# The decode attention's 16 products go from GpSimd to VectorE and start one weight tile later

## The chip, the cores and the metric

The kernel runs on one core of one Trainium2 chip. A core has TensorE (PE, with its weight loads shown as PEld), VectorE (DVE), ScalarE (ACT), GpSimd (POOL) and SyncE (SP). Each engine works through its own instruction stream in order and waits on semaphores for the others. Here SP only issues DMAs. The metric is the device time of one execution in microseconds (us), smaller being better; the median of several runs is compared. The trace of one execution shows instructions, what each waited for, the clock granted to TensorE, and DMA traffic.

## What is computed

One step of a two-layer decoder, for a prompt group (1024 tokens) and a sample group (8 sequences with one new token each) that share the weights. Layer 0 puts dilated window attention and a state space scan side by side; layer 1 is a matrix memory mixer. The change touches one piece of layer 0: the attention of the 8 new tokens over their cached keys and values.

```python
def dilated_attention_sample(q, k, v, k_buf, v_buf):
    kk = jnp.concatenate([k_buf.astype(k.dtype), k], axis=1)
    vv = jnp.concatenate([v_buf.astype(v.dtype), v], axis=1)
    ...
    for window, dil in DILATION_PATTERNS:
        ...
        s = jnp.einsum('bthe,btjhe->bthj', q, kg, preferred_element_type=jnp.float32)
        s = jnp.where(valid[None, :, None, :], s, -jnp.inf)
        lse = jax.nn.logsumexp(s, axis=-1)
        p = jnp.exp(s - lse[..., None])
        outs.append(jnp.einsum('bthj,btjhe->bthe', p.astype(v.dtype), vg))
        lses.append(lse)
    return combine_by_denominator(outs, lses)
```

In the kernel a partition holds one of 64 pairs of sequence and head, with one of two halves of the cached rows that any pattern reaches: 128 partitions, 128 rows each, 64 values per row. All is float32.

## The kernel before, in words

Layer 0 runs in this order. First the q, k and v projections (tiles `pq`). Then a loop over 12 weight tiles f of the state space branch (L698 on). For each f it takes a weight tile `w` (loaded by SP to `raw`, L95; rounded by ScalarE to `wh`, L90; the remainder `wl` by VectorE, L91), runs three column blocks c of 24 matmuls each (`pf`, L112), copies them out on ScalarE (`craw`, L242), and then runs a 4-tap convolution: the first tap on ScalarE (L248), three on VectorE (L250), the activation on ScalarE (L254) with its product on VectorE (L255). After it a second loop of 12 tiles (gates), in which the state space scan runs (`sE`, from L730), then the output projection.

Two other streams are handed out between the column blocks of the first loop:

- `att_pump` steps, only in f = 0 to 5, and the rest in one go at f = 5: the prompt attention's remaining blocks. TensorE makes scores `pS` (L428); VectorE adds the mask and finds the extremum (L433, reading PSUM); ScalarE takes the exponential (L434); statistics `ast` go through DRAM and back as `aot` (L441 to L443); VectorE combines them (`aft`, L448 to L456) and scales the probabilities `P` (L468); TensorE transposes them (`pT`, L470); VectorE or ScalarE copies them to `PT` (L475, L473); TensorE multiplies with the values (`pO`, L487).
- `dpump` steps, one per column block: the decode attention, 19 steps in the queue `dq`. `dec_prep` loads the new queries, keys and values (`q_b`, `k_b`, `v_b`, L628). Eight `dec_k` steps each load 128 x 1024 cached keys to `dk` (L632), multiply them in place with the query (L634, GpSimd) and sum over 64 values (L635, VectorE) to 16 scores of `dsc`. `dec_soft` makes the softmax. Eight `dec_v` steps do the like with the cached values, `dv` (L649), the product with the probabilities (L651, GpSimd) and the sum over 128 rows (L652, VectorE). `dec_fin` joins the halves through DRAM.

The tiles `dk`, `dv` and later `sE` share one pool of three buffers (tag "E"), so a fourth load waits until a sum has released a buffer; all these loads go out on SP in SP's order. The result is read by `dec_fin2` (L676, tile `pda`) at f = 1 of the second loop.

The order of a queue is not the order in which the code emits: the framework plans each engine's stream ahead, takes an instruction when its operands are ready in its plan and the engine is free there, and among several ready ones the earliest in the code. So steps that depend on little stand far ahead of their place in the code. The position in the code acts as a rank.

Of the kernel before, what the change touches and what calls it, by code (L numbers as in the profile page):

```python
# [28 lines left out]
def body(ctx, tc, I, O):  # L29
    nc = tc.nc  # L30
    V, A, G, PE = nc.vector, nc.scalar, nc.gpsimd, nc.tensor
    mult, add, sub, mx, mn = ALU.mult, ALU.add, ALU.subtract, ALU.max, ALU.min
# [23 lines left out]
    def S(name, dt=F32):  # L56
        return slab.tile([128, 1040], dt, tag="S", name=name)
# [4 lines left out]
    def EP(name, dt=F32):  # L62
        return cur["ep"].tile([128, 1040], dt, tag="E", name=name)
# [19 lines left out]
    def C(name, shape, src=None, p=None):  # L83
        t = (p or cur["cst"]).tile(shape, F32, name=name)
        if src is not None:
            load(t, src)
        return t
# [27 lines left out]
    class Weights:  # L115
# [8 lines left out]
        def load(self, ahead=1):  # L124
            while len(self.raws) < min(ahead, len(self.srcs)):
                self.raws.append(raw_load(*self.srcs[len(self.raws)]))
# [112 lines left out]
    def conv_c(w, xh, xl, c, raw, samp, side=()):  # L239
        p = proj_c(w, xh, xl, c, side)  # L240
        if c < 2:
            A.copy(raw[:, 3 + c * CH : 3 + (c + 1) * CH], p[:, :CH])  # L242
        else:
            A.copy(raw[:, 3 + 2 * CH : 3 + NP], p[:, : CH - 8])
            A.copy(samp, p[:, CH - 8 : CH])

    def conv_taps(raw, o, w4, b1, tail):
        A.activation(o[:, :NP], raw[:, 0:NP], AF.Identity, bias=b1, scale=w4[:, 0:1])  # L248
        for j in range(1, 4):
            V.scalar_tensor_tensor(o[:, :NP], raw[:, j : j + NP], w4[:, j : j + 1], o[:, :NP], mult, add)  # L250
        G.tensor_scalar(tail, raw[:, NP : NP + 3], 1.0, None, mult)

    def conv_act(raw, o):
        A.activation(raw[:, :NP], o[:, :NP], AF.Tanh)  # L254
        V.scalar_tensor_tensor(o[:, :NP], raw[:, :NP], 1.0, o[:, :NP], add, mult)  # L255

    def conv_raw(raw=None):
        raw = S("craw") if raw is None else raw
        G.memset(raw[:, 0:3], 0.0)
        return raw  # L260
# [250 lines left out]
    def att_pump(n, limit):  # L511
        for _ in range(n):
            if attq and attq[0][0] < limit:
                attq.popleft()[1]()
# [80 lines left out]
    def dt_prep():  # L595
        V.tensor_tensor(dtr, dtr, dtb.unsqueeze(1).broadcast_to([128, 9, 16]), add)
        softplus_neg(dtf, 144, False)
        A.activation(alog, alog, AF.Exp)
        V.tensor_scalar(alog, alog, -1.0, None, mult)
        V.tensor_tensor(dta, dtr, alog.unsqueeze(1).broadcast_to([128, 9, 16]), mult)  # L600
        pac = X("pac")
        PE.matmul(pac[:, 0:128], tri, dtaf[:, 0:128], start=True, stop=True)
        PE.matmul(pac[:, 128:256], ones, dtaf[:, 0:128], start=True, stop=True)
        PE.matmul(pac[:, 256:384], dtaf[:, 0:128], tri, start=True, stop=True)
        V.tensor_copy(acum, pac[:, 0:128])
        V.tensor_scalar(nacum, acum, -1.0, None, mult)
        V.tensor_tensor(wl, pac[:, 128:256], acum, sub)
        A.activation(wl, wl, AF.Exp)
        V.tensor_tensor(wl, wl, dtf[:, 0:128], mult)
        A.activation(dec, pac[:, 128:256], AF.Exp)  # L610
        act_sb = smg.tile([128, 128], F32, tag="dg", name="act_sb")
        V.tensor_copy(act_sb, pac[:, 256:384])
        store(acd, act_sb)
# [3 lines left out]
    q_b = C("q_b", [128, 64])  # L617
    k_b = C("k_b", [128, 64])
    v_b = C("v_b", [128, 64])
    dsc = C("dsc", [128, 129])  # L620
# [9 lines left out]
    def dec_k(j):  # L630
        t = EP("dk")
        load(t[:, :1024], I["ck"][:, j * 1024 : j * 1024 + 1024])  # L632
        tv = t[:, :1024].rearrange("p (a b) -> p a b", b=64)
        G.tensor_tensor(tv, tv, q_b.unsqueeze(1).broadcast_to([128, 16, 64]), mult)  # L634
        V.reduce_sum(dsc[:, j * 16 : j * 16 + 16], tv, AX.X)  # L635

    def dec_soft():
# [9 lines left out]
    def dec_v(j):  # L647
        t = EP("dv")
        load(t[:, :1024], I["cv"][:, j * 1024 : j * 1024 + 1024])  # L649
        tv = t[:, :1024].rearrange("p (a b) -> p a b", b=128)  # L650
        G.tensor_tensor(tv, tv, dsc[:, 0:128].unsqueeze(1).broadcast_to([128, 8, 128]), mult)  # L651
        V.reduce_sum(dao[:, j * 8 : j * 8 + 8], tv, AX.X)  # L652

    def dec_fin():
# [23 lines left out]

    dq = deque([dec_prep])
    dq.extend(lambda j=j: dec_k(j) for j in range(8))  # L680
    dq.append(dec_soft)
    dq.extend(lambda j=j: dec_v(j) for j in range(8))
    dq.append(dec_fin)

# [3 lines left out]
    def dpump(n):  # L688
        for _ in range(n):
            if dq:  # L690
                dq.popleft()()
# [7 lines left out]
    for f in range(12):  # L699
        w = wq0.next()  # L700
        raw = conv_raw()
        o = S("cout")
        for c in range(3):
            conv_c(w, xh, xl, c, raw, xbs[:, f])
            if c == 1 and later:
                later.popleft()()
            if f < 6:
                att_pump(3, 4)
            if f > 3:
                dpump(1)  # L710
        conv_taps(raw, o, scw[:, f], scb[:, f : f + 1], cvo[:, f])
        later.append(lambda raw=raw, o=o: conv_act(raw, o))
        xbc.append(o)
        if f == 5:
            att_pump(80, 4)
        if f == 7:
            dt_prep()
# [1146 lines left out]
```

## Time and profile before

| | |
|---|---|
| median of 3 runs | 2164.42 us (2162.53 to 2165.84) |
| the profiled execution | 2158.71 us, of which the span of the trace is 2156.9 us |
| PE busy | 2097.2 us, 97% of the span |
| DVE busy | 1350.3 us, 63% |
| ACT busy | 849.6 us, 39% |
| POOL busy | 561.9 us, 26% |
| mean granted TensorE clock | 0.994 of full speed |

How to read it: times are from the span's start. Busy is the time in which at least one instruction of the engine ran. A bracket behind an instruction tells how long its engine stood idle just before it and what ended that. A clock of 1.00 is the upper of the two levels, 2.4 GHz, and 0.50 is the lower, 1.2 GHz; a figure between is a mean over a stretch that has both. A wait for several semaphores is put down to the one that came last.

### The profile page before, as it was taken

What the parts mean: (1) busy time and instruction counts of PE and PEld (TensorE: products, weight loads), DVE (VectorE), ACT (ScalarE), POOL (GpSimd) and SP (SyncE); (2) the same over time, 40 slices, a digit from 0 to 9 for tenths busy, and PEclk for the clock granted to TensorE, in tenths of its full rate; (3) what the DMA queues carried; (4) which work ended last, traced back from release to release, by engine and by line L of the source; (5) the groups of instructions that cost most, each with busy time, mean ns of one, the idle gap of its engine ahead of it and who ended that gap; (6) DMA issues with size and microseconds to landing.
All of it is one profiled execution on the core that took longest, in us unless ns stands there. A gap on an engine that the chain in (4) does not pass through costs nothing.

```text
span 2156.9 us, 35181 instructions
## 1 busy us (share of the span) xinstructions
PE 2097.2 (97%) x12926; PEld 1880.9 (87%) x12926; DVE 1350.3 (63%) x3176; ACT 849.6 (39%) x1837; POOL 561.9 (26%) x1052
## 2 busy tenths in 40 slices
PE   7999989999999999999999999999999999999998
PEld 6877777997898899989989899898898998987798
DVE  7444388768778655645548566575565665746844
ACT  5434334454425434433425334253343443524421
POOL 4222144015540002142141321413214223141000
PEclk9999999999999999999999999999999999999999
DMA  4222053125555552411214133132231232416852
GB/s 160 72 73 78 26 156 97 47 94 169 184 169 179 178 178 77 99 40 47 89 34 151 44 97 116 37 115 78 84 131 29 92 106 68 142 30 199 280 169 94
DMA packets 162076, 232.29 MB, mean 108 GB/s; under 512 B 41200, under 2 KB 106976, under 8 KB 161904
## 3 DMA queue, kind: packets, MB, share of 16 engines
q1 hardware_dynamic: 161904, 230.04, 34.0%
q8 instruction: 102, 1.67, 0.3%
q14 instruction: 70, 0.57, 0.1%
HBM read 174.35 MB, written 55.62 MB: 107 GB/s over the span
## 4 chain that ended last, share of the span: by engine, by line
PE 78%; DVE 7%; DMA 3%; POOL 3%; issue 2%; ACT 2%; POOLq 0%; SPq 0%; DVEq 0%; ACTq 0%
PE pf L112 32%; PE pvo L112 16%; PE po L931 14%; PE pq L112 4%; PE mN L112 2%; PE mC L112 2%; PE pS L428 1%; PE pO L487 1%; PE mS L1294 1%; PE pT L470 1%; DMA sE<-acd 1%; POOL mCl L91 1%; DVE P L468 1%; PE mH L1355 1%; PE mS L1296 1%
## 5 line engine op out<-in xcount | busy, mean ns | idle before, releaser
L112 PE MATMUL pf<-yh,wh 128*128 128x344 f32 x1152 | 370.1, 321 | 0.0
L112 PE MATMUL pf<-yl,wh 128*128 128x344 f32 x1152 | 368.9, 320 | 0.0
L112 PE MATMUL pf<-yh,wl 128*128 128x344 f32 x1152 | 368.5, 320 | 0.0
L91 DVE TENSOR_TENSOR wl<-raw,wh 128x1024 fp32r<-128x1024 f32 x128 | 161.7, 1263 | 156.3 <-ACT wh L90 155.7
L90 ACT CAST wh<-raw 128x1024 fp32r<-128x1024 f32 x128 | 133.9, 1047 | 254.8 <-PE pf L112 93.6
L112 PEld LDWEIGHTS pf<-yh,wh 128*128 128x128 f32 x1152 | 216.9, 188 | 1.3 <-ACT craw L242 1.0
L112 PEld LDWEIGHTS pf<-yl,wh 128*128 128x128 f32 x1152 | 216.5, 188 | 0.0
L112 PEld LDWEIGHTS pf<-yh,wl 128*128 128x128 f32 x1152 | 216.4, 188 | 0.0
L112 PE MATMUL pvo<-wvh,yh 128*128 128x512 f32 x512 | 206.0, 402 | 0.0
L112 PE MATMUL pvo<-wvh,yl 128*128 128x512 f32 x512 | 201.9, 394 | 0.0
L112 PE MATMUL pvo<-wvl,yh 128*128 128x512 f32 x512 | 201.7, 394 | 0.0
L112 PE MATMUL pf<-xh,wh 128*128 128x344 f32 x576 | 195.4, 339 | 0.8 <-ACT gth L236 0.8
L112 PE MATMUL pf<-xh,wl 128*128 128x344 f32 x576 | 188.0, 326 | 0.0
L112 PE MATMUL pf<-xl,wh 128*128 128x344 f32 x576 | 187.9, 326 | 0.0
L1282 DVE TENSOR_SCALAR mx<-mx,mbs,md 128x256 f32<-128x256 f32 x64 | 26.4, 413 | 176.7 <-POOL md L1281 176.7
L250 DVE SCALAR_TENSOR_TENSOR cout<-craw,mcw,cout 128x1024 f32<-128x1024 f32 x96 | 123.1, 1284 | 13.4 <-ACT cout L248 11.9
L931 PE MATMUL po<-oh,wl 128*128 128x512 f32 (+2 forms) x384 | 122.9, 320 | 1.6 <-DVE wl L91 1.6
L931 PE MATMUL po<-oh,wh 128*128 128x512 f32 (+2 forms) x384 | 123.0, 321 | 0.9 <-ACT oh L90 0.9
L931 PE MATMUL po<-ol,wh 128*128 128x512 f32 (+2 forms) x384 | 123.0, 321 | 0.0
L112 PEld LDWEIGHTS pf<-xh,wh 128*128 128x128 f32 x576 | 110.5, 192 | 7.6 <-issue 5.9
L112 PEld LDWEIGHTS pvo<-wvh,yl 128*128 128x128 f32 x512 | 96.1, 188 | 22.3
L112 PEld LDWEIGHTS pf<-xl,wh 128*128 128x128 f32 x576 | 110.7, 192 | 4.3 <-issue 4.3
(440 smaller groups left out, 5030.3 us busy)
## 6 DMA issues: line engine op xcount, KB each, us to landing
raw<-in_wo SPq DMA_DIRECT2D x56, 512.0 KB
raw<-in_wq SPq DMA_DIRECT2D x32, 512.0 KB
raw<-in_wvo SPq DMA_DIRECT2D x32, 512.0 KB
dC<-in_mcs SPq DMA_DIRECT2D x32, 512.0 KB
out_mcs<-dC SPq DMA_DIRECT2D x32, 512.0 KB
raw<-in_wf SPq DMA_DIRECT2D x24, 512.0 KB
sE<-acd SPq DMA_DIRECT2D x16, 512.0 KB
raw<-in_wz SPq DMA_DIRECT2D x16, 512.0 KB
```

What stands on the lines that cost most here:

```text
L90: A.copy(hi, src)
L91: eng.tensor_tensor(lo, src, hi.bitcast(F32), sub)
L112: PE.matmul(out, l, r, start=i == 0, stop=i == n - 1)
L250: V.scalar_tensor_tensor(o[:, :NP], raw[:, j : j + NP], w4[:, j : j + 1], o[:, :NP], mult, add)
L428: PE.matmul(p[:, :n], qT[g][hs, qs], kT[g][hs, ks], start=True, stop=True)
L468: V.tensor_scalar(P, P, u["f"][:, kind, x, h : h + 1], None, mult)
L470: PE.transpose(pt[:, h * n + k : h * n + k + 128], P[:, k : k + 128], ident)
L487: PE.matmul(po[h * 64 : h * 64 + 64, qs], v, PT[:, h * n + k * 128 : h * n + k * 128 + 128], start=j + k == 0, stop=j == 7 and k == nk - 1)
L931: PE.matmul(p[:, :m], wt[:, ws], at, start=i == 0 and q == 0, stop=i == nk - 1 and q == 2)
L1282: V.tensor_scalar(x, x, bs[:, 6:7], d[:, 2:3], sub, mult)
L1294: PE.matmul(pS[:, 0:128], hd["k"][j][:, tok], hd["q"][j][:, tok], start=j == 0, stop=j == 1)
L1296: PE.transpose(pS[:, 128 + j * 128 : 256 + j * 128], hd["k"][j][:, tok], ident)
```

## The change

The two products of the decode attention are issued on VectorE (`V`) in place of GpSimd (`G`), each directly in front of its sum, and the `dpump` steps in the first loop begin at f = 5 in place of f = 4. That loop then calls `dpump` 21 times where it called it 24 times; the queue holds 19 steps at that point, so all are still issued inside it, the last one at f = 11. Shapes, data, buffers, loads and results stay.

```diff
@@ -631,7 +631,7 @@
         t = EP("dk")
         load(t[:, :1024], I["ck"][:, j * 1024 : j * 1024 + 1024])
         tv = t[:, :1024].rearrange("p (a b) -> p a b", b=64)
-        G.tensor_tensor(tv, tv, q_b.unsqueeze(1).broadcast_to([128, 16, 64]), mult)
+        V.tensor_tensor(tv, tv, q_b.unsqueeze(1).broadcast_to([128, 16, 64]), mult)
         V.reduce_sum(dsc[:, j * 16 : j * 16 + 16], tv, AX.X)
@@ -648,7 +648,7 @@
         t = EP("dv")
         load(t[:, :1024], I["cv"][:, j * 1024 : j * 1024 + 1024])
         tv = t[:, :1024].rearrange("p (a b) -> p a b", b=128)
-        G.tensor_tensor(tv, tv, dsc[:, 0:128].unsqueeze(1).broadcast_to([128, 8, 128]), mult)
+        V.tensor_tensor(tv, tv, dsc[:, 0:128].unsqueeze(1).broadcast_to([128, 8, 128]), mult)
         V.reduce_sum(dao[:, j * 8 : j * 8 + 8], tv, AX.X)
@@ -706,7 +706,7 @@
                 later.popleft()()
             if f < 6:
                 att_pump(3, 4)
-            if f > 3:
+            if f > 4:
                 dpump(1)
```

## Rows read from the trace of the kernel before

**Rows 1.** The page's first part: busy time, share of the span and number of instructions of each engine.

```profile
PE 2097.2 (97%) x12926; PEld 1880.9 (87%) x12926; DVE 1350.3 (63%) x3176; ACT 849.6 (39%) x1837; POOL 561.9 (26%) x1052
```

**Rows 2.** The table by stretch, all engines: the stretch, its length, busy us (and instructions) of PE, PEld, DVE, ACT and POOL, then granted clock, DMA share and GB/s. 272 to 390 holds the decode attention, 390 to 500 what follows it; the last two rows are parts of the first.

```profile
272.00:390.00 118.00, 107.72 (x676) 89.15 (x676) 101.09 (x204) 49.04 (x125) 48.17 (x30) 0.94 0.38 111
390.00:500.00 110.00, 109.96 (x751) 106.03 (x747) 77.00 (x107) 52.13 (x113) 14.60 (x23) 1.00 0.28 91
...
350.00:370.00 20.00, 20.00 (x118) 15.07 (x117) 16.23 (x33) 7.18 (x20) 7.77 (x5) 1.00 0.16 55
370.00:390.00 20.00, 19.82 (x154) 17.40 (x154) 18.08 (x46) 10.05 (x20) 0.27 (x2) 1.00 0.18 43
```

**Rows 3.** The table by stretch, PE alone, around four gaps: stretch, length, busy us of PE, granted clock, DMA share, GB/s.

```profile
286.00:296.00 10.00, 6.16 (x36) 0.83 0.31 63
298.00:306.00 8.00, 6.63 (x45) 0.79 0.58 184
328.00:338.00 10.00, 8.12 (x38) 0.83 0.05 7
340.00:350.00 10.00, 7.41 (x45) 0.83 0.65 182
```

**Rows 4.** The timeline of PE: start, duration, engine, line, instruction, and the idle time in front of it with its releaser. The first matmul of the loop's tile f = 0 here, then the instructions that end the four gaps.

```profile
274.13 0.42 PE L112 MATMUL pf<-xh,wh 128*128 128x344 f32 x1
...
290.51 1.12 PE L487 MATMUL pO<-PT,vt 128*64 128x128 f32 x8 [3.84 <-DVE PT L475]
...
300.46 1.78 PE L487 MATMUL pO<-PT,vt 128*64 128x128 f32 x16 [1.37 <-DVE PT L475]
...
330.27 0.70 PE L428 MATMUL pS<-kT,qT 64*128 64x256 f32 x2 [1.88 <-DVE ast L433]
...
343.99 0.33 PE L470 MATMUL pT<-ident,P 128*128 128x128 f32 x1 [2.59 <-DVE P L468]
```

**Rows 5.** The timeline of POOL, some of the 16 products.

```profile
285.85 2.38 POOL L634 TENSOR_TENSOR dk<-dk,q_b 128x1024 f32<-128x1024 f32 x1 [0.76 <-DMA dk<-in_ck]
296.32 2.40 POOL L634 TENSOR_TENSOR dk<-dk,q_b 128x1024 f32<-128x1024 f32 x1 [8.09 <-DMA dk<-in_ck]
...
326.21 9.23 POOL L651 TENSOR_TENSOR dv<-dv,dsc 128x1024 f32<-128x1024 f32 x3 [3.68 <-ACT dsc L645]
...
364.73 4.75 POOL L651 TENSOR_TENSOR dv<-dv,dsc 128x1024 f32<-128x1024 f32 x2 [11.95 <-DMA dv<-in_cv]
```

**Rows 6.** The timeline of DVE, single instructions and runs of like ones between 282 and 345.

```profile
282.45 6.71 DVE L468 TENSOR_SCALAR P<-P,aft 128x256 f32<-128x256 f32 x9
...
289.77 0.68 DVE L475 COPY PT<-pT 128x512 f32<-128x512 f32 x1
...
296.69 3.11 DVE L91 TENSOR_TENSOR wl<-raw,wh 128x1024 fp32r<-128x1024 f32 x1 [1.76 <-ACT wh L90]
299.73 0.68 DVE L475 COPY PT<-pT 128x512 f32<-128x512 f32 x1
...
320.65 1.22 DVE L635 TENSOR_REDUCE dsc<-dk 128x16 f32<-128x1024 f32 x1 [2.45 <-POOL dk L634]
...
341.64 3.02 DVE L468 TENSOR_SCALAR P<-P,aft 128x128 f32<-128x128 f32 x4
```

**Rows 7.** Groups by line and shape, DVE: busy us and mean ns of one, then idle time in front and its releasers. The first six are of 272 to 390, the last two of 390 to 500, where POOL does little.

```profile
L250 DVE SCALAR_TENSOR_TENSOR cout<-craw,scw,cout 128x1024 f32<-128x1024 f32 x14 | 25.5, 1825 | 1.2 <-ACT cout L248 1.2
L468 DVE TENSOR_SCALAR P<-P,aft 128x256 f32<-128x256 f32 x38 | 14.8, 456 | 0.1
L652 DVE TENSOR_REDUCE dao<-dv 128x8 f32<-128x1024 f32 x8 | 9.6, 1211 | 2.0 <-POOL dv L651 2.0
...
L91 DVE TENSOR_TENSOR wl<-raw,wh 128x1024 fp32r<-128x1024 f32 x6 | 9.2, 1536 | 1.8 <-ACT wh L90 1.8
...
L468 DVE TENSOR_SCALAR P<-P,aft 128x128 f32<-128x128 f32 x10 | 6.5, 693 | 0.0
L255 DVE SCALAR_TENSOR_TENSOR cout<-craw,cout 128x1024 f32<-128x1024 f32 x4 | 6.3, 1574 | 1.3 <-ACT craw L254 1.2
...
L250 DVE SCALAR_TENSOR_TENSOR cout<-craw,scw,cout 128x1024 f32<-128x1024 f32 x23 | 30.4, 1320 | 2.4 <-ACT cout L248 2.0
L91 DVE TENSOR_TENSOR wl<-raw,wh 128x1024 fp32r<-128x1024 f32 x9 | 11.3, 1258 | 16.0 <-ACT wh L90 16.0
```

**Rows 8.** The table by stretch, DVE's instructions of one line alone: the first row is L468, the other two are L250. Stretch, length, busy us and instructions, clock, DMA share, GB/s.

```profile
370.00:390.00 20.00, 4.45 (x16) 1.00 0.18 43
...
301.00:313.20 12.20, 7.15 (x3) 0.87 0.40 126
...
325.00:338.00 13.00, 7.59 (x3) 0.87 0.22 63
```

**Rows 9.** The timeline of SP's queue: DMA issues of the first and of two later cache tiles, and of the first `sE`.

```profile
272.29 0.35 SPq L632 DMA_DIRECT2D dk<-in_ck  x1
...
291.09 0.50 SPq L632 DMA_DIRECT2D dk<-in_ck  x1
...
360.97 1.41 SPq L649 DMA_DIRECT2D dv<-in_cv  x2
...
432.83 1.28 SPq L730 DMA_DIRECT2D sE<-acd  x3
```

**Rows 10.** The timeline of PE: the first instruction that reads the decode attention's result.

```profile
496.80 0.41 PE L676 MATMUL pda<-ident,do 8*128 8x8 f32 x4
```

## The prediction, made before the change was run

> **What bounds the kernel now.** I read the engines' busy times first: TensorE is busy 97% of the span, VectorE 63%, GpSimd 26% [rows 1]. So a change on VectorE or GpSimd counts only where TensorE stands still or runs at the lower clock. The table by stretch says where that is near this change: from 272 to 390 us TensorE is busy 107.7 of 118 us at a granted clock of 0.94, VectorE 101.1 of 118, GpSimd 48.2. From 390 to 500 TensorE is busy throughout at 1.00, and VectorE only 77 of 110 [rows 2].
>
> The table around the four gaps sizes the loss. PE is idle 3.84, 1.37, 1.88 and 2.59 us, 9.7 in all. After each gap the clock falls from 2.4 to 1.2 GHz for a while: 0.17 x 10, 0.21 x 8, 0.17 x 10 and 0.17 x 10 are 1.7 us of lost time each [rows 3]. Together 16.5 us: the most that this stage can give back. The timeline of PE names what each gap waits for: a copy to `PT`, another, the statistics `ast` and the scaled `P`, all on VectorE [rows 4]. So VectorE is late, and the third step is to ask why.
>
> The timelines of VectorE and GpSimd side by side show it. Nine scalings of `P` take 6.71 us from 282.45 on [rows 6], with a product on GpSimd from 285.85 to 288.23 [rows 5]; later sixteen take 4.45 us, 0.28 each [rows 8]. `wl` takes 3.11 us at 296.69, beside the product at 296.32, and 1.22 to 1.26 where GpSimd is quiet [rows 5 to 7]. While GpSimd multiplies, some of VectorE's instructions are held: scalings, taps, remainders. The sums L652 are not, 1.211 us [rows 7].
>
> **The change part by part.**
>
> *What VectorE gains.* Per line, against an unhindered price. Taps L250: 25.5 us less 14 x 1.28 (a tap's usual duration, under the mean of 1.32 outside, which still holds a hindered one) is 7.6. Scalings L468: 14.8 + 6.5 less 48 x 0.28 is 7.9. Remainders L91: 9.2 less 6 x 1.22 is 1.9. Activations L255: 6.3 less 4 x 1.22 is 1.4. Sum 18.8 us [rows 7, 8].
>
> *What VectorE gets.* No row shows this product on VectorE. The nearest is `wl`, a two-input tensor operation of the same 128 x 1024 in float32, 1.22 us at best and 1.26 on average [rows 7]. Bounds: 1.21 (the sum of such a tile, a one-input pass, rows 7) and 2.4 (the product on GpSimd, rows 5). I take 1.22, since shape, type and engine agree: 16 x 1.22 = 19.5 us. So VectorE's work in the stage stays the same, 101.1 - 18.8 + 19.5 = 101.8 us. The gain, if any, comes from where the work lies, and from VectorE no longer waiting for GpSimd (2.45 us once, 2.0 another time, 4.4 in all) [rows 6, 7].
>
> *Where it lies.* I walk the stage and compare how much earlier VectorE and TensorE arrive. Products go directly in front of their sums; loads and the other engines stay in order.
>
> 282 to 301: the nine scalings need 2.5 us, so VectorE reaches the copy of 289.77 4.2 us earlier, before PE asks for it: the first gap goes, 3.84 + 1.7 = 5.5. Then two products stand in front of two sums (+2.4), `wl` is 1.9 shorter, and the 1.76 us that VectorE waited for `wh` there are filled. The copy at 299.73 is 4.2 - 2.4 + 1.9 + 1.8 = 5.5 earlier, and so is PE [rows 4, 6]. The second gap stays. Credit 5.5.
>
> 301 to 325: six products, 7.3. Three taps in 7.15 us become 3.8 (rows 8), an activation saves 0.9, a wait of 2.45 for GpSimd goes (rows 6): 6.7. VectorE is 4.9 early, PE 5.5.
>
> 325 to 338: three taps in 7.59 us become 3.8 [rows 8], an activation saves 0.5. About 2.0 of this lies ahead of the third gap, whose statistics come 6.9 earlier where PE is 5.5 earlier: of 1.88 us about 0.5 is left, and I count its clock loss as gone. PE is 5.5 + 1.4 + 1.7 = 8.6 earlier, VectorE 4.9 + 4.3 = 9.2.
>
> 338 to 345: three products of `dv` (3.7) come ahead of the scalings at 341.64, which take 1.1 in place of 3.02 [rows 6]. VectorE ends 9.2 - 3.7 + 1.9 = 7.4 earlier. The fourth gap, 2.59 us, therefore grows by 1.2, and its clock loss stays. Credit 7.4.
>
> 345 to 390: five products, 6.1, against the remaining 2.3 of the 18.8, the wait of 2.0, and the free time of VectorE, 20 - 16.2 and 20 - 18.1, of which that wait is a part [rows 2]. TensorE has no gap of note there. I charge nothing; if the cover fails, up to 2 us.
>
> Sum: 7.4 us. Bounds: 0, if VectorE's unchanged 102 us bind PE as today, and 16.5, if all four gaps and their clock losses go.
>
> *One tile later.* The order in the code is a rank, not a time: the first `dk` load is issued at 272.29, before the first matmul of tile f = 0 at 274.13 [rows 4, 9], although the code of before puts it at f = 4. I expect the steps to stay far ahead of their place, with a little more of them behind the attention. I cost this at nothing. Bounds: it takes nothing, or moves some products behind 390, where VectorE has 33 us free [rows 2], which is part of the 16.5. What hides a delay at the far end: the result is read at 496.8 [rows 10], 127 us after the last sum, which follows the products of 364.73 [rows 5]; the next user of the three buffers, `sE`, is loaded at 432.83 [rows 9], some 60 us later.
>
> *What is queued behind.* A product on VectorE waits for its load, as GpSimd did, but behind VectorE's wait stand scalings, masks and copies for which PE waits. GpSimd waited 0.76, 8.09 and 11.95 us for loads [rows 5] at no cost to anyone. SP's queue is not passed by anything new; a load still waits for a sum, and SP's later issues behind it.
>
> *A rule against it.* VectorE is busy 101.1 us and GpSimd 48.2 in this stage [rows 2]. The Trainium skill, Perfetto Trace Analysis, section Identifying the Most-Contended Engine, says to take an engine's occupancy as the measure and to relieve the busiest first; by that, moving work from an engine at 41% to one at 86% is the wrong way. The trace disagrees in one point: 18.8 us of the occupancy are time held, not work [rows 7, 8]. What becomes of the time if that point is wrong is the fourth rival.
>
> **The rivals.**
>
> *All gaps go.* The products find VectorE's free moments or slide behind 390, and PE never waits long enough to lose its clock. For it: 17 us of idle VectorE in the stage today, 33 after it [rows 2]. Against: the pairs of 2.4 us sit in one piece in front of what PE waits for. 16.5 us, the time would be 2158.7 - 16.5 = 2142.2 in the profiled execution.
>
> *No gain.* VectorE's 102 us bind PE as they do today; the gaps move to other places. For it: the sum of VectorE's work does not change. Against: the largest gap comes from nine scalings ahead of which no product stands. 2158.7, or 3 us less.
>
> *VectorE waits for loads (slower).* After the first three tiles, 13 loads can be issued only when a sum frees a buffer. A load issued at 291.09 let its product start at 296.32, 5.2 us later; one at 360.97 at 364.73, 3.8 later [rows 5, 9]. Two other pairs on VectorE cover 4.9 us of that. If the planner believes in faster loads and leaves only one pair (2.4) between, each load holds VectorE 1.4 to 2.8 us: 18 to 36 us over 13 loads, against the credit of 7.4: 2170 or more. It decides from 0.6 us per load. Against it: VectorE has other work between pairs in nearly every stretch. A few such waits I expect.
>
> *VectorE becomes the bound (slower).* If the long instructions are long for another reason, the 18.8 us stay and the stage needs 101.1 + 19.5 = 120.6 us of VectorE. With all its idle time filled that is 2.6 us more than today's 118; with the 17 us of idle kept, 19.5 more: 2161 to 2178. Both are worked from the busy time of the stage [rows 2]. It decides from the point where less than 2.6 us of the holding goes away. The short scalings after 370 [rows 8], where GpSimd works 0.27 us [rows 2], speak against it.
>
> *It does not do what it says*: the planner leaves the products behind other work so that the sums, and the buffers, come much later. The slack of 60 us covers that.
>
> **How the numbers follow.** Profiled execution: 2158.71, its span 2156.9 and 1.8 around it. 2158.7 - 7.4 = 2151.3. The median of the runs, 2164.42, lies 5.7 above that execution (0.3%); I keep the difference, so the forecast is 2164.4 - 7.4 = 2157.0 us. In the same terms: all gaps go 2147.9; no gain 2161 to 2165; waits for loads 2175 and more; VectorE the bound 2167 to 2184.
>
> Chances: the forecast, 3 to 12 us gained, 0.52; nearly all gaps go 0.13; no gain 0.21; waits for loads 0.10; VectorE the bound 0.03; not what it says 0.01. The measurement tells about 0.2% from no change, 4.3 us. So faster by more than that 0.62 (the first two less a small part), within it 0.23, slower 0.15. The range from 2149 to 2168 leaves out some 2 in 10, most of it the slower rivals, at the low end a part of the rival in which all gaps go.
>
> **What the changed profile would show.** L468 at 0.28 us each and L250 at 1.28 everywhere in the stage, or the holding was not GpSimd's doing. Products on VectorE at 1.22 us. PE's first gap gone, others smaller; granted clock in the stage above 0.94. VectorE's busy time near 101 us, in a stage some 7 us shorter. If VectorE shows waits for `dk` or `dv` loads above 7 us in all, the slower rival is right; if L468 and L250 are short and PE still loses 16 us, the no-gain one. The forecast is wrong too if the planner reorders a later stage, which nothing here touches.

## The result, and the profile after

The changed kernel takes 2146.51 us (median of 5 runs, 2144.85 to 2149.32), the kernel before 2164.42 (2162.53 to 2165.88): ratio 0.9921, 95% interval 0.991 to 0.9932. That is 17.9 us gained, more than twice the 7.4 of the forecast, and 2.5 us below the low end of its range. The profiled execution is the one of 2146.51, its span 2144.6 us.

Read the stages first. The table takes the start of the first matmul of each (in the timeline of PE) as its border, for the second row that of the last of the 864 matmuls of the first loop. The 273 to 274 us ahead of the first loop are left out. Beside the two kernels it has three of the runs that are described below.

| stage, us | before | after | e2 | e4 | e7 |
|---|---|---|---|---|---|
| first loop (decode attention inside) | 195.9 | 178.8 | 198.6 | 180.1 | 197.3 |
| second loop (scan) | 216.3 | 221.0 | 220.3 | 220.5 | 218.7 |
| output projection | 142.7 | 142.7 | 142.7 | 142.7 | 143.1 |
| layer 1, main part | 1126.2 | 1126.4 | 1126.6 | 1126.1 | 1126.3 |
| what follows it | 201.6 | 202.2 | 202.7 | 203.8 | 202.2 |

The whole gain, 17.1 us, lies in the first loop. The second loop goes from 216.3 to 221.0, which hides 4.7 of it between the two traces: over the nine traces with the scan unchanged it takes 216 to 221 us, with the products on either engine. In e2, whose engines run the instructions of the kernel before in the same order, it takes 220.3, so 4 us here are a difference between executions. They are likely most of the 5.7 us by which the profiled execution of before lies under its median; the medians show the gain whole.

The page's first line of the changed kernel, busy times and instructions:

```profile
PE 2094.1 (98%) x12926; PEld 1878.8 (88%) x12926; DVE 1346.1 (63%) x3192; ACT 849.8 (40%) x1837; POOL 515.6 (24%) x1036
```

VectorE has 16 instructions more and 4 us less of busy time than in [rows 1]. The table by stretch, columns as in [rows 2]; the last two rows are places of gaps [rows 3]:

```profile
272.00:390.00 118.00, 117.59 (x798) 100.30 (x798) 103.54 (x221) 54.83 (x135) 4.48 (x16) 1.00 0.42 120
...
390.00:500.00 110.00, 108.14 (x744) 102.21 (x743) 86.53 (x132) 55.13 (x129) 24.41 (x34) 1.00 0.31 103
286.00:296.00 10.00, 9.86 (x80) 8.51 (x75) 9.99 (x14) 3.56 (x6) 0.28 (x2) 1.00 0.62 156
...
340.00:350.00 10.00, 10.00 (x57) 7.43 (x57) 6.86 (x20) 3.95 (x14) 0.00 (x0) 1.00 0.00 0
```

TensorE works 117.59 of 118 us at clock 1.00, where it worked 107.72 at 0.94 [rows 2]. That makes the sum by itself: idle time 10.28 to 0.41, and 0.06 x 118 = 7.1 us of clock, together 17. All four gaps of [rows 4] are gone. VectorE's busy time is hardly changed, 103.54 for 101.09, but it now holds more work: the same stretch has 798 of PE's matmuls where it had 676.

Groups by line and shape, DVE, 272 to 390, columns as in [rows 7]:

```profile
L250 DVE SCALAR_TENSOR_TENSOR cout<-craw,scw,cout 128x1024 f32<-128x1024 f32 x17 | 21.7, 1274 | 0.0
L468 DVE TENSOR_SCALAR P<-P,aft 128x256 f32<-128x256 f32 x38 | 10.6, 343 | 0.0
L91 DVE TENSOR_TENSOR wl<-raw,wh 128x1024 fp32r<-128x1024 f32 x8 | 9.8, 1222 | 0.2 <-ACT wh L90 0.2
...
L634 DVE TENSOR_TENSOR dk<-dk,q_b 128x1024 f32<-128x1024 f32 x8 | 9.5, 1217 | 0.0
...
L651 DVE TENSOR_TENSOR dv<-dv,dsc 128x1024 f32<-128x1024 f32 x7 | 8.4, 1219 | 0.6 <-ACT dsc L645 0.6
L652 DVE TENSOR_REDUCE dao<-dv 128x8 f32<-128x1024 f32 x6 | 7.2, 1203 | 0.0
...
L468 DVE TENSOR_SCALAR P<-P,aft 128x128 f32<-128x128 f32 x10 | 2.3, 283 | 0.0
```

Mean taps fall from 1825 to 1274 ns, remainders from 1536 to 1222, the smaller scalings from 693 to 283. The 38 larger scalings take 10.6 us of busy time, 0.28 each, where they took 14.8 (single records overlap, so their mean, 343 ns, is longer). The products take 1.22 us each. No product waits for a load: the only idle time in front of one is 0.6 us, for the softmax.

Now the place, which the forecast got wrong. The timeline of DVE where the first two gaps were:

```profile
281.77 2.45 DVE L468 TENSOR_SCALAR P<-P,aft 128x256 f32<-128x256 f32 x9
...
284.83 0.68 DVE L475 COPY PT<-pT 128x512 f32<-128x512 f32 x1
285.43 1.91 DVE L468 TENSOR_SCALAR P<-P,aft 128x256 f32<-128x256 f32 x7
287.27 2.35 DVE L634 TENSOR_TENSOR dk<-dk,q_b 128x1024 f32<-128x1024 f32 x2
289.54 1.21 DVE L635 TENSOR_REDUCE dsc<-dk 128x16 f32<-128x1024 f32 x1
290.67 0.68 DVE L475 COPY PT<-pT 128x512 f32<-128x512 f32 x1
291.26 1.21 DVE L91 TENSOR_TENSOR wl<-raw,wh 128x1024 fp32r<-128x1024 f32 x1
```

The nine scalings take 2.45 us, where they took 6.71 [rows 6]. The copy at 284.83 is the one that ended the first gap (289.77 before), the copy at 290.67 the one that ended the second (299.73 before). This second copy has two products and one sum ahead of it. In the kernel before it stood behind two sums, a wait and `wl`; the wait and `wl` are in [rows 6], and these are the sums, in the timeline of DVE of the kernel before:

```profile
292.21 1.20 DVE L635 TENSOR_REDUCE dsc<-dk 128x16 f32<-128x1024 f32 x1
...
293.72 1.21 DVE L635 TENSOR_REDUCE dsc<-dk 128x16 f32<-128x1024 f32 x1
```

In the changed kernel `wl` and the second sum come after the copy: the two products went in, and two other things went out. The copy is 9 us earlier. Further on, in the changed kernel:

```profile
337.39 1.26 DVE L468 TENSOR_SCALAR P<-P,aft 128x128 f32<-128x128 f32 x6
...
347.92 2.36 DVE L651 TENSOR_TENSOR dv<-dv,dsc 128x1024 f32<-128x1024 f32 x2 [0.56 <-ACT dsc L645]
```

The first `dv` products stand at 347.92, behind the scalings, and 21.7 us later than GpSimd began them [rows 5]. The forecast had three of them in front. TensorE's order has moved as well: counted in its timelines, the transposition that ended the fourth gap follows 237 matmuls of this loop, where it followed 218.

### The profile page after: what moved, and what is told of

It reads as the page before. It is cut to its first block, busy times and chain, and to the rows that moved or that the text cites. A ratio compares the mean times of both kernels' runs of the same rounds, so it can differ in the third digit from the quotient of the medians.

```text
span 2144.6 us, 35154 instructions
## 1 busy us (share of the span) xinstructions
PE 2094.1 (98%) x12926; PEld 1878.8 (88%) x12926; DVE 1346.1 (63%) x3192; ACT 849.8 (40%) x1837; POOL 515.6 (24%) x1036
## 4 chain that ended last, share of the span: by engine, by line
PE 78%; DVE 6%; DMA 3%; POOL 3%; issue 2%; ACT 2%; SPq 0%; POOLq 0%; DVEq 0%; ACTq 0%
PE pf L112 32%; PE pvo L112 16%; PE po L931 14%; PE pq L112 4%; PE mN L112 2%; PE mC L112 2%; PE pS L428 2%; PE pO L487 1%; PE mS L1294 1%; PE pT L470 1%; POOL mCl L91 1%; PE mH L1355 1%; PE mS L1296 1%; DMA mE<-mud 1%; POOL dso L841 1%
## 5 line engine op out<-in xcount | busy, mean ns | idle before, releaser
L250 DVE SCALAR_TENSOR_TENSOR cout<-craw,mcw,cout 128x1024 f32<-128x1024 f32 x96 | 123.0, 1282 | 13.2 <-ACT cout L248 11.7
L112 PEld LDWEIGHTS pvo<-wvh,yh 128*128 128x128 f32 x512 | 96.3, 188 | 20.8 <-issue 1.3
```

The costliest lines, as they stand in the source:

```text
L112: PE.matmul(out, l, r, start=i == 0, stop=i == n - 1)
```

## The experiments

The theory, from the prediction: GpSimd's products hold some of VectorE's instructions, VectorE is late for what TensorE waits for, and TensorE loses the gap and its clock. The first rival: the start one tile later makes the gain. The second rival: VectorE is overfull in any case, and its 19.5 us of products must cost something. Behind them stood a question of size: why 17 us and not 7.4. All runs were timed against the kernel before on the same chip (medians 2163.18, 2164.59 and 2164.88 us in the three groups e1 to e4, e5 to e8, e9 to e11). Diffs are against the changed kernel.

### e1 and e2: engine and start apart

e1 keeps the products on VectorE and takes the start back:

```diff
-            if f > 4:
+            if f > 3:
```

> Products on VectorE, steps starting at f = 4 again (only the start undone). Theory A, GpSimd's products hold VectorE and that alone costs the time: as the changed kernel, 2146.5 us within 0.2%. Theory B, the later start is what helps: 2155 to 2164 us, with gaps of PE back in the stage from 272 to 390. I expect A.

e2 keeps the later start and takes the products back to GpSimd:

```diff
-        V.tensor_tensor(tv, tv, q_b.unsqueeze(1)...
+        G.tensor_tensor(tv, tv, q_b.unsqueeze(1)...
...
-        V.tensor_tensor(tv, tv, dsc[:, 0:128].unsqueeze(1)...
+        G.tensor_tensor(tv, tv, dsc[:, 0:128].unsqueeze(1)...
```

> Products on GpSimd as before, steps starting at f = 5 (only the start changed). Theory A: as the kernel before, 2164 us within 0.2%, the four gaps of 9.7 us in all at the same places. Theory B: 2147 to 2155 us. I expect A. It also shows how far one profiled execution of this order strays from the median.

e1: 2146.34 us, ratio 0.9926 (0.9914 to 0.9938), the changed kernel's time. e2: 2166.2, ratio 1.0012 (1.0002 to 1.0023), the time of before, or 2 to 3 us above it. The traces tell why: on every engine e2 runs the instructions of the kernel before, in the same order, and e1 those of the changed kernel. The first loop takes 180.7 us in e1 and 198.6 in e2, where the long gaps are 4.12, 1.49, 1.89 and 2.66 us, at the same instructions as before. The start does nothing, and the first rival falls: all of the gain is the engine's.

### e3: GpSimd works again, without anyone needing it

The changed kernel, with each tile multiplied once more by GpSimd behind its sum. The second product is used by nobody.

```diff
         V.reduce_sum(dsc[:, j * 16 : j * 16 + 16], tv, AX.X)
+        G.tensor_tensor(tv, tv, q_b.unsqueeze(1).broadcast_to([128, 16, 64]), mult)
...
         V.reduce_sum(dao[:, j * 8 : j * 8 + 8], tv, AX.X)
+        G.tensor_tensor(tv, tv, dsc[:, 0:128].unsqueeze(1).broadcast_to([128, 8, 128]), mult)
```

> The changed kernel, in which GpSimd multiplies each dk or dv tile once more after its sum has been taken; nobody reads that product, but the tile's buffer is released only after it (2.4 us later). The decode attention's result is that of the changed kernel. VectorE's order of instructions is that of the changed kernel up to the fourth product of dv. Theory A (holding): L468 and L250 get long again beside these products, PE has gaps after VectorE's instructions, 2155 to 2168 us. Theory C (the gain comes from the products' new place in VectorE's order, not from the holding): 2145 to 2150 us. I expect A, about 2160.

2169.67 us, ratio 1.0029 (1.0017 to 1.004): all of the gain is lost, and 6 us more. The timeline of DVE, and under it that of POOL for the same time (an added product has the line of its sum, L635 or L652):

```profile
296.55 1.27 DVE L250 SCALAR_TENSOR_TENSOR cout<-craw,scw,cout 128x1024 f32<-128x1024 f32 x1
...
297.95 3.20 DVE L250 SCALAR_TENSOR_TENSOR cout<-craw,scw,cout 128x1024 f32<-128x1024 f32 x1
...
308.44 1.21 DVE L635 TENSOR_REDUCE dsc<-dk 128x16 f32<-128x1024 f32 x1
309.57 1.91 DVE L634 TENSOR_TENSOR dk<-dk,q_b 128x1024 f32<-128x1024 f32 x1
311.41 2.41 DVE L639 TENSOR_TENSOR dnk<-q_b,k_b 128x64 f32<-128x64 f32 x1
```

```profile
296.70 3.36 POOL L635 TENSOR_TENSOR dk<-dk,q_b 128x1024 f32<-128x1024 f32 x1 [3.49 <-DVE dsc L635]
308.01 5.73 POOL L635 TENSOR_TENSOR dk<-dk,q_b 128x1024 f32<-128x1024 f32 x2 [7.94 <-DVE dsc L635]
```

Read the ends. GpSimd's product of 296.70 meets a tap in progress and takes 3.36 us, 1 us over its 2.4 [rows 5]. It ends at 300.06; the tap that started at 297.95 ends at 301.15, 1.1 later, near a whole tap's 1.28. So each engine seems to wait for the other's instruction and then do its own in full. The product of 128 x 64 elements takes 2.41 us and ends with GpSimd's second product (313.82 and 313.74). The sum of 308.44, beside the same GpSimd work, keeps its 1.21. One reservation: the tiles are also freed later, four `dk` loads in a row held SP's queue from 300.09 for 17.7 us, and loads behind them came late. So e3 shows the holding, but its 23 us (2169.67 - 2146.51) need not all be the holding's.

The order of the queues is what makes e3 a test. Up to 376 us VectorE has the instructions of the changed kernel in the same order, and TensorE up to 388 us. Yet TensorE has four gaps before 345 us, 1.29, 1.19, 1.56 and 4.60, where the changed kernel has none, so a new place in a queue can't be their cause. The longest, in the timelines of PE, DVE and POOL:

```profile
341.11 0.48 PE L470 MATMUL pT<-ident,P 128*128 128x128 f32 x1 [4.60 <-DVE P L468]
```

```profile
338.70 3.08 DVE L468 TENSOR_SCALAR P<-P,aft 128x128 f32<-128x128 f32 x4
```

```profile
337.70 3.27 POOL L635 TENSOR_TENSOR dk<-dk,q_b 128x1024 f32<-128x1024 f32 x1 [1.33 <-issue]
```

The same four scalings in the changed kernel, in the timeline of DVE:

```profile
330.22 1.01 DVE L468 TENSOR_SCALAR P<-P,aft 128x128 f32<-128x128 f32 x4
```

They take 3.08 us beside GpSimd's product and 1.01 without it, and among VectorE's waits from 272 to 420 us none is for a load.

The Trainium skill, SBUF — State Buffer, section SBUF: two separate sides, says that VectorE and GpSimd share one pair of ports as an exclusive lock, which a VectorE instruction needs in a two-port mode, or with two SBUF inputs against a GpSimd instruction that reads SBUF, and that the loser blocks for the whole instruction. The trace agrees for the tap and the two-input products, and for the one-input sum, which isn't held. The scalings have one tile as input and are held [rows 6]; whether they run in such a mode, no run here shows.

### e4: the changed kernel without its products

The 16 products are left out, so the decode attention's scores and values are not multiplied; loads and sums stay. Nothing is issued in their place, on either engine.

```diff
-        V.tensor_tensor(tv, tv, q_b.unsqueeze(1)...
+        pass
...
-        V.tensor_tensor(tv, tv, dsc[:, 0:128].unsqueeze(1)...
+        pass
```

> The changed kernel with the 16 products left out altogether (the sums run over the unmultiplied cache tiles, so the decode attention's result is another). It asks what the 16 x 1.22 = 19.5 us on VectorE still cost. Theory A with room on VectorE: nothing, 2144 to 2149 us. Theory D (VectorE binds the stage, as my walk through the gaps had it): 5 to 9 us less than the changed kernel, 2138 to 2142. I expect A, as PE has no gap left that VectorE ends.

2149.2 us, ratio 0.9933 (0.9921 to 0.9946); the first loop takes 180.1 us, with the products 178.8. So leaving the products out gains nothing: their 19.5 us on VectorE cost nothing where they stand now. The second rival falls. One limit is that the planner made another order without them, with a gap of 1.2 us in TensorE, so two orders are compared and not one.

### e5 and e6: half each

e5 has the `dk` products on VectorE and the `dv` products on GpSimd, e6 the reverse (the one or the other line of e2's diff).

> The changed kernel with the eight dk products on VectorE and the eight dv products back on GpSimd. Theory (GpSimd's products hold VectorE's two-input and scaling instructions, and each held stretch in front of a copy, a scaling or a statistic for which TensorE waits makes a gap): the gaps made beside dk products (the first two of the kernel before, 3.84 + 1.7 and 1.37 + 1.7, 8.6 us) are gone, those beside dv products (1.88 + 1.7 and 2.59 + 1.7, 7.9 us) stay: 2146.5 + 7.9 = 2154.4, within 2151 to 2158. Rival (it takes only that enough work leaves GpSimd, or that the dv products have room): 2146 to 2149. In the trace scalings L468 and taps L250 should be long only from some 326 us on.

> The mirror: dv products on VectorE, the eight dk products back on GpSimd. Theory: the gaps beside dk products stay (8.6 us), those beside dv products go: 2146.5 + 8.6 = 2155.1, within 2152 to 2159; with the run before this one, the two losses add up to the whole difference of 17 us. Rival (one long held stretch alone decides, the nine scalings of the first gap, and the others follow from it): this one 2160 or more, and the run with dk on VectorE near 2147.

e5: 2157.88 us, ratio 0.9963 (0.9951 to 0.9976), 6.7 us gained. e6: 2153.0, ratio 0.9947 (0.9934 to 0.996), 11.6 gained. Together 18.3, the 17.9 of the whole change. Both lie in the ranges that the theory gave, e5 at the upper end, and the rivals' times don't fit. The split by gaps (8.6 for `dk`, 7.9 for `dv`) was the wrong way round: against the changed kernel the `dk` products on GpSimd cost 6.5 us (e6) and the `dv` products 11.4 (e5). The traces show a reason. In e6 the first gap is back to the hundredth, with the nine scalings, but the second is not; one of 1.02 us stands further on. The timelines of PE and DVE:

```profile
289.97 1.12 PE L487 MATMUL pO<-PT,vt 128*64 128x128 f32 x8 [3.84 <-DVE PT L475]
```

```profile
281.87 6.75 DVE L468 TENSOR_SCALAR P<-P,aft 128x256 f32<-128x256 f32 x9
```

In e5 the `dv` products make one gap in a new place, longer than any of before. PE, DVE and POOL:

```profile
378.10 1.12 PE L470 MATMUL pT<-ident,P 128*128 128x128 f32 x4 [9.22 <-DVE P L468]
```

```profile
364.66 2.29 DVE L250 SCALAR_TENSOR_TENSOR cout<-craw,scw,cout 128x1024 f32<-128x1024 f32 x1
366.88 2.37 DVE L448 TENSOR_TENSOR aft<-ast,aot 128x16 f32<-128x16 f32 x1
369.27 2.26 DVE L449 TENSOR_TENSOR aft<-aft,ast 128x16 f32<-128x16 f32 x1
```

```profile
363.41 8.09 POOL L651 TENSOR_TENSOR dv<-dv,dsc 128x1024 f32<-128x1024 f32 x3 [0.88 <-DMA dv<-in_cv]
```

Two combinations of 128 x 16 elements take 2.37 and 2.26 us beside three products in a row, and the scalings come after them. In the timeline of DVE of the changed kernel the first of them is:

```profile
323.05 0.17 DVE L448 TENSOR_TENSOR aft<-ast,aot 128x16 f32<-128x16 f32 x1
```

The tap and the two combinations are held for 5.3 us in all. The rest of the 9.22 is other work of VectorE that stands before the scalings; its order differs from the changed kernel's from some 350 us on.

### e7: the same work, in another place

This run asks where the 7.4 came from. The products and sums stay on VectorE, but are ranked above the attention's and the convolution's work, so that they stand as early as their loads allow.

```diff
-        V.tensor_tensor(tv, tv, q_b.unsqueeze(1)...
-        V.reduce_sum(dsc[:, j * 16 : j * 16 + 16], tv, AX.X)
+        with tc.high_priority(): V.tensor_tensor(tv, tv, q_b.unsqueeze(1)...
+        with tc.high_priority(): V.reduce_sum(dsc[:, j * 16 : j * 16 + 16], tv, AX.X)
...
```

(and the same for `dv`)

> The changed kernel with each product and its sum raised in the order of planning above the attention's and the convolution's work, so that they stand as early in VectorE's queue as their loads allow, in one piece, ahead of copies and scalings. It tests the step of the forecast that kept two gaps: products directly in front of what TensorE waits for. Theory A (that step's mechanism was right and only the place was not): pairs of 2.4 us ahead of copies and scalings make TensorE wait again, 1.2 to 2.6 us a gap and a low-clock stretch of 3.4 us behind each, of which half is lost: 2151 to 2160. Theory B (only holding by GpSimd makes gaps; a pair's place does not matter): 2145 to 2149.

2163.18 us, ratio 0.9992 (0.9981 to 1.0003): no gain at all, though GpSimd does little in the stage, and a larger loss than either expectation had. The table by stretch and the group of taps, then PE's two longest gaps, then what DVE did before the first of them:

```profile
272.00:390.00 118.00, 107.63 (x661) 88.08 (x660) 97.54 (x213) 48.01 (x123) 6.30 (x14) 0.91 0.36 109
```

```profile
L250 DVE SCALAR_TENSOR_TENSOR cout<-craw,scw,cout 128x1024 f32<-128x1024 f32 x13 | 16.6, 1278 | 0.1
```

```profile
350.28 0.48 PE L470 MATMUL pT<-ident,P 128*128 128x128 f32 x1 [4.75 <-DVE P L468]
352.92 0.70 PE L487 MATMUL pO<-PT,vt 128*64 128x128 f32 x4 [2.16 <-DVE PT L475]
```

```profile
344.13 2.50 DVE L651 TENSOR_TENSOR dv<-dv,dsc 128x1024 f32<-128x1024 f32 x2 [0.24 <-DMA dv<-in_cv]
346.56 2.34 DVE L652 TENSOR_REDUCE dao<-dv 128x8 f32<-128x1024 f32 x2
348.81 1.21 DVE L651 TENSOR_TENSOR dv<-dv,dsc 128x1024 f32<-128x1024 f32 x1
349.95 0.28 DVE L468 TENSOR_SCALAR P<-P,aft 128x128 f32<-128x128 f32 x1
```

Taps are short (1278 ns), GpSimd does 6.3 us, and TensorE still stands 10.4 us (10.3 in the kernel before) and runs at 0.91 (0.94 before). Five instructions of the decode attention in a row stand ahead of one scaling of 0.28 us for which TensorE waits. So "products in front of what PE waits for" can cost as much as the whole gain; the changed kernel has it nowhere. This holds for the place of the walk's fourth gap alone. Where its second gap would be, TensorE has none in e7, though products and sums stand ahead of that copy: the planner moved TensorE's order too, and the multiplication that waits for the copy follows 108 matmuls of the loop, 79 in the kernel before.

### e8 to e11: the same in the second loop

There the new tokens' scan has two products per half tile on GpSimd (L839 and L841, 128 x 512) around a step on VectorE. e8 moves the second, e10 the first, e9 both; e11 both and the prompt's additions of L791.

```diff
-            G.tensor_tensor(ov, xd[:, 4 * u : 4 * u + 4]..., B_b..., mult)   # L839: e9, e10, e11
+            V.tensor_tensor(ov, xd[:, 4 * u : 4 * u + 4]..., B_b..., mult)
             V.scalar_tensor_tensor(tu, tu, dsc2[:, 1:2], o, mult, add)
-            G.tensor_tensor(ov, tv, C_b..., mult)                            # L841: e8, e9, e11
+            V.tensor_tensor(ov, tv, C_b..., mult)
```

> The changed kernel, and in the second loop the scan's product of the sample group (128 x 512 by the row C) on VectorE in place of GpSimd. If the same holding makes gaps there, the stage (216 to 221 us in the runs so far) gives back 2 to 6 us: 2141 to 2145. If TensorE's gaps there come from the chain itself or from elsewhere: 2146 to 2149, no difference; if VectorE's longer queue delays the second loop's convolution: slower.

> The changed kernel, and both products of the sample group's scan step (128 x 512 each, by the rows B and C) on VectorE. With the product by C alone moved, the time was 2139.0 and VectorE still stood 8.9 us between 500 and 640 us for the product by B on GpSimd. If that wait and the holding that is left are in TensorE's way: 2133 to 2138. If VectorE's 16 x 0.67 = 10.7 us more of work now bind it in this stage (it was busy 92% from 500 to 600): 2139 to 2145.

> The changed kernel with the product by B alone on VectorE, the one by C left on GpSimd. Tells which of the two products cost the stage its time. If GpSimd's load as such counts (18.9 us of this product against 23.8 us of the other): a gain of some 5 us, 2141 to 2143. If it is the product by C, behind which the state's step and the sum wait in the same step: 2145 to 2149, no difference.

> Both scan products and the small additions of the prompt's scan output (L791, 128 x 128, 56 of them) on VectorE, so that GpSimd does next to nothing there. VectorE gets some 15 us more. If only relief from GpSimd counted: as the run with both scan products or 1 to 2 us less. If VectorE is by then the bound of the stage: 3 to 12 us slower than that run.

| | time, us | ratio to before | 95% interval |
|---|---|---|---|
| changed kernel | 2146.51 | 0.9921 | 0.991 to 0.9932 |
| e8, L841 | 2139.03 | 0.9873 | 0.9857 to 0.989 |
| e10, L839 | 2142.85 | 0.9889 | 0.987 to 0.9908 |
| e11, both and L791 | 2145.61 | 0.9903 | 0.9884 to 0.9922 |
| e9, both | 2150.42 | 0.9923 | 0.9905 to 0.9941 |

e8 beats both kernels: 25.6 us below the 2164.59 of the kernel before, some 7.5 below the changed one. e10 points the same way, so it is not the product by C alone. Moving both gives nothing over the changed kernel. Of the times expected, e10's was met; e8 came out below its range, e9 above both of its ranges, and e11 faster than e9 by more than was expected. The table by stretch, 500 to 600, of the changed kernel, of e8, of e9 and of e11:

```profile
500.00:600.00 100.00, 90.26 (x611) 79.54 (x609) 77.64 (x135) 43.46 (x121) 52.55 (x66) 0.93 0.53 169
```

```profile
500.00:600.00 100.00, 92.08 (x667) 81.58 (x668) 92.02 (x154) 45.29 (x125) 43.55 (x58) 0.98 0.56 177
```

```profile
500.00:600.00 100.00, 86.89 (x597) 77.59 (x596) 82.93 (x139) 42.22 (x119) 35.53 (x45) 0.93 0.52 157
```

```profile
500.00:600.00 100.00, 93.72 (x673) 83.59 (x673) 96.83 (x197) 41.74 (x119) 11.36 (x9) 0.98 0.54 167
```

One idea for e9 was that VectorE becomes the bound. It is less busy there (82.93) than in e8 (92.02), and e11, with VectorE at 97%, is the faster of the two. The waits of PE from 480 to 680, of e8 and of e9, show what does differ:

```profile
PE pcb L745 <- ACT sbt L749: 6.2, 4, 2.6
```

```profile
PE pcb L745 <- ACT sbt L749: 14.3, 5, 4.0
```

In e9 TensorE waits 14.3 us in five gaps for a copy `sbt` that ScalarE makes. The changed kernel has 7.7 us of this wait; e11 has 0.6, but 10.5 for another product of ScalarE, `gth`. What makes these late wasn't settled; that it is again the place in a queue is a guess.

## Why the prediction was too small

**What bounds the kernel.** Right. VectorE was late because GpSimd's products held its instructions: 17 us of the gain lie in that loop, they vanish with GpSimd's products back (e2), and splitting these splits them (e5, e6).

**What VectorE gains and gets.** Right. Products were put at 1.22 us and took 1.22; scalings at 0.28 and taps at 1.28, measured 0.28 and 1.27; VectorE's busy time near 101, measured 103.54, with more of the convolution inside the stretch.

**Where it lies.** This step failed: "Products go directly in front of their sums; loads and the other engines stay in order." The walk put products in the places of the old sums and left the rest of VectorE's queue, and TensorE's, as it was. It so kept the second gap (1.37 + 1.7), 0.5 of the third and a longer fourth (2.59 + 1.2 + 1.7), and came to 7.4. In the new queue the copy of the second gap overtakes `wl` and a sum, the `dv` products stand behind the scalings, and TensorE does 19 more matmuls of the loop before it needs the fourth gap's scalings. No gap is kept: 17.1 us between the traces' first loops, 17.9 between medians. The cost itself was no fancy. e7 builds the place that the walk had imagined for the fourth gap, and worse, and loses all of the gain. The error was to take one order, of which no row could tell, as the forecast, when the order alone was worth from 0 to 17 us. That the trace of before showed where GpSimd's results were used said nothing of where VectorE would take the products. Why the planner chose this order stays open.

**One tile later.** Right: nothing (e1, e2). Not even the "little more of them behind the attention" came; the order is the same.

**The rivals.** "All gaps go" was the case, at 16.5 us and 2147.9, 1.4 above the measured time. Its chance of 0.13 rested on the same imagined pairs, and the range began at 2149, above its time. A bound that the text itself had worked out was cut off: the end of the range should have been below 2147.9. "No gain", "waits for loads" and "VectorE becomes the bound" are refuted by the waits and by e4. The Trainium skill, Perfetto Trace Analysis, section Identifying the Most-Contended Engine, says to optimize first the engine with the highest occupancy. The measurement goes the other way than the prediction's reading of that rule: the 17.9 us came from loading the busier of the two engines.

**From the trace to the median.** Keeping the 5.7 us between them was right as far as the traces tell: some 4 of them are the short second loop of that execution, which the change doesn't touch.

## What to carry to other kernels

Read the durations of one instruction shape with the neighbour engine busy and quiet before trusting a busy share: 18.8 us of VectorE's work here were time held, and taking the neighbour's products over cost nothing more (e4). When a planner places moved work, the order is not known beforehand; work out the best and the worst place, and let the range reach both. And do it one product at a time: in the second loop the one product gained 7.5 us, the other 3.7, both together nothing.

## What was unexpected of the hardware

A held instruction's time depended less on its size than on the end of GpSimd's product: 128 x 16 elements took 2.37 and 2.26 us beside GpSimd's products (e5) and 0.17 in the changed kernel, 128 x 64 took 2.41 (e3), and held taps of 128 x 1024 took 2.29 (e5) and 3.20 (e3). Small steps therefore lose most for their size: in e5 two of them added 4.3 us ahead of the 9.22 us gap's end.
